# Column-wise substitution in the RWKV base blocks, and the transposes of q and k drained by ScalarE alone

## The chip, the cores and the metric

The kernel runs on one core of a Trainium2 chip. The core has five engines with instruction queues of their own: TensorE (PE; its weight loads are listed as PEld), VectorE (DVE), ScalarE (ACT), GpSimd (POOL) and SyncE (SP), which here only issues DMA transfers. The metric is the device time of one execution in microseconds; a time is the median of several executions. Beside it there is one profiled execution, whose span runs from the first to the last instruction.

## The reference

One decoder layer over 1024 prompt tokens and 8 x 8 sampled tokens: one input projection is split among an RWKV-7 group, a short convolution and stick-breaking attention, and an output projection, an MLP and a gated embedding follow. Two pieces matter here. The RWKV-7 state is a recurrence over the tokens:

```
def step(s, inp):
    r_t, w_t, k_t, v_t, a_t, b_t = inp
    sa = jnp.einsum('bhvk,bhk->bhv', s, a_t)
    s = (s * w_t[:, :, None, :] + sa[..., None] * b_t[:, :, None, :]
         + v_t[..., None] * k_t[:, :, None, :])
    y = jnp.einsum('bhvk,bhk->bhv', s, r_t)
```

And the queries and keys of the attention (8 heads of 64) are normalised and get a gain for each position in the head:

```
q = rmsnorm(q, lw['q_gain'])
k = rmsnorm(k, lw['k_gain'])
...
z = jnp.einsum('bqhd,bkhd->bhqk', q_blk.astype(jnp.float32), kf) * scale + bias_f
```

Everything is float32. TensorE's products of large matrices are made of two parts for each operand, a rounded high part and the remainder (names with h and l).

## The kernel before, in words

**The recurrence in chunks.** The 1024 tokens are 16 chunks of 64. Inside a chunk the recurrence is a unit triangular system, and the kernel inverts its matrix for each chunk and head. For a half j of the heads (two heads, j = 0 and 1), `wkv_products` makes the matrices on TensorE (L260) in three groups of 8, 8 and 1 chunks (the last is the sampled tokens), multiplies them by a triangular mask into the tile LT (VectorE, L262; two buffers), and stores them to `l_s` in memory. After j = 1, `wkv_base` loads the diagonal blocks of 32 x 32 of all 16 chunks, 4 heads and 2 blocks: 128 blocks, one on each partition, the tile base_Z (L276). The substitution that inverts them runs in VectorE: for row i a product of i x i elements (L281) into base_Q and a sum over its last axis (L283) into row i of base_X, for i from 1 to 31. One operand of the product is base_X read transposed. Then L284 writes the transposed inverse, and L285 stores both to `t_s`. The sampled tokens go through the same function later with blocks of 16.

**Around it.** For each j, the lines L425 to L443 make the remaining streams: aa and kx (L425, L426), pinv (L427, stored), r times the decay (rx, stored), rx times the bonus weights and kx (L436), and the bonus itself (L442 on TensorE, L443 on VectorE). The tiles of this phase share buffers, among them one group of 12, so a later tile waits for the last reader of an earlier one.

**The attention's projection.** `project` makes q, k and v for two halves of the heads (hf), in groups of 256 tokens (i0): 48 matmuls a group (L791 to L793) into a PSUM bank (two banks, in turn), a copy into the tile nat (ScalarE, L798; five buffers), the square (ScalarE, L801), its sum (VectorE, L803), a root and a reciprocal (L804, L805) and the product (VectorE, L806). `keep` writes k and v out (GpSimd multiplies k by its gain, L816). `stack` transposes q and k of a group on TensorE (L840, four transposes) into one PSUM bank, of which there is one; ScalarE writes the rounded high part times the gain to sth (L842), VectorE the remainder to stl (L843), and four DMA issues, two on ScalarE's queue and two on SyncE's, store them (L846). sth, stl and the tile spl of v share four buffers. There are 16 stacks, and a stack is put behind the last matmul of a later group.

**The local step of the chunks.** `wkv_local` takes the chunks in pairs: SyncE loads ar, bk (L483, L486) and TT, the blocks of `t_s` (L491). TensorE multiplies (L508) and transposes, VectorE masks (L511), L539 and L544 put the off-diagonal part together, L552 adds it into TT, and L560 and L562 apply TT. `wkv_chain` then steps over the chunks one after another (L621 to L638), and the attention follows.

**What sets the order.** The program is written as one sequence; a scheduler that simulates the times orders the instructions on each engine, and each engine then runs its own list strictly in order. A wait of one instruction holds all that stand behind it on its engine. `tc.issue_after(x)` makes the scheduler put what is inside behind the instruction x. Since TensorE can do the projection matmuls at almost any time, the scheduler puts them between the small products of the chunks.

Of the kernel before, what the change touches and what calls it, by code (L numbers as in the profile page):

```python
# [21 lines left out]
F32 = mybir.dt.float32  # L22
F32R = mybir.dt.float32r
I32 = mybir.dt.int32
AF = mybir.ActivationFunctionType
ALU = mybir.AluOpType
AX = mybir.AxisListType
# [21 lines left out]
def hybrid_step(ctx: ExitStack, tc: tile.TileContext, I, O):  # L49
    nc = tc.nc  # L50
    V, S, G, PE, SP = nc.vector, nc.scalar, nc.gpsimd, nc.tensor, nc.sync
# [4 lines left out]
    def f(t):  # L56
        return t.bitcast(F32)
# [79 lines left out]
    def P1(name, i=0):  # L137
        return par[:, col[name] + i:col[name] + i + 1]
# [42 lines left out]
    for i in range(9):  # L181
# [4 lines left out]
        xt, r = xts[i]  # L186
# [7 lines left out]
        for g in range(2):  # L194
            pt = tr().rearrange("p (k t) -> p k t", k=4)
            for k in range(4):
                c = (4 * g + k) * 128
# [19 lines left out]
    pt = tr()  # L217
# [8 lines left out]
    mfull = km.tile([128, 2, 2, 64], F32, name="mfull")  # L226
    G.memset(mfull, 1.0)
    for s in range(2):
        hs = slice(64 * s, 64 * s + 64)
        for q in range(2):  # L230
            for kind in range(2):
                m = mfull[hs, q, kind, :]
# [18 lines left out]
    def wkv_products(j, am, bm):  # L251

        for c0 in (0, 8, 16):
            n = min(8, 17 - c0)
            p3 = tr()[:, :n * 64].rearrange("p (c t) -> p c t", c=n)
            for c in range(n):
                for s in range(2):
                    hs = slice(64 * s, 64 * s + 64)
                    q = slice((c0 + c) * 64, (c0 + c) * 64 + 64)
                    PE.matmul(p3[hs, c, :], bm[hs, q], am[hs, q], start=True, stop=True)  # L260
            LT = bp.tile([128, 8, 64], F32, name="LT", bufs=2)
            V.tensor_mul(LT[:, :n], p3, mfull[:, c0 // 16, 1, None, :].to_broadcast([128, n, 64]))  # L262
            c = c0 % 16
            for s in range(2):
                SP.dma_start(l_s[c0 // 16][c:c + n, 2 * j + s].rearrange("c i t -> i c t"), LT[64 * s:64 * s + 64, :n])

    def wkv_base(pool, nc_, BS, l_s, t_s, tags=("Z", "X", "Q"), bufs=(1, 1, 1)):
        na = 64 // BS
        np_ = nc_ * 4
        P_ = slice(0, na * np_)  # L270
        Z = pool.tile([128, BS, BS], F32, name="base_Z", tag=tags[0], bufs=bufs[0])
        X = pool.tile([128, 2, BS, BS], F32, name="base_X", tag=tags[1], bufs=bufs[1])
        Q = pool.tile([128, BS * BS], F32, name="base_Q", tag=tags[2], bufs=bufs[2])
        blocks = l_s.rearrange("c h (a r) (b t) -> a b (c h) r t", a=na, b=na)
        for a in range(na):
            SP.dma_start(Z[a * np_:(a + 1) * np_], blocks[a, a])  # L276
        G.memset(X[P_, 1], 0.0)
        G.memset(X[P_, 1].rearrange("p r t -> p (r t)")[:, 0:BS * BS:BS + 1], 1.0)
        for i in range(1, BS):
            q = Q[P_, 0:i * i].rearrange("p (c j) -> p c j", c=i)  # L280
            V.tensor_mul(q, Z[P_, 0:i, i][:, None, :].to_broadcast([na * np_, i, i]),  # L281
                         X[P_, 1, 0:i, 0:i].rearrange("p j c -> p c j"))
            V.reduce_sum(X[P_, 1, i, 0:i], q, axis=AX.X)  # L283
        V.tensor_copy(X[P_, 0], X[P_, 1].rearrange("p r t -> p t r"))  # L284
        SP.dma_start(t_s.rearrange("a c h k r t -> (a c h) k r t"), X[P_])  # L285


# [2 lines left out]
    def pe_tile(name, dtype=F32):  # L290
        return rp.tile([128, LW], dtype, name=name, tag="pe", bufs=12)
# [14 lines left out]
    pt = tr()  # L306
# [7 lines left out]
    last = rp.tile([9, 1024], F32, name="last")  # L314

    def rw_tile(w, m, ct):

        raw = pe_tile("raw")
        xs = pe_tile("xs")
        G.memset(raw[:, 0:1], 0.0)  # L320
        rs3 = raw[:, E1:E1 + NB * 9].rearrange("p (b j) -> p b j", j=9)
        G.tensor_copy(rs3[:, :, 0], shT[:, ct, :])
        for t0, n in CH:
            ps = acc()
            gemm_t(ps, w, m, hT, t0, n)
            np_ = min(n, NP - t0)
            S.copy(raw[:, 1 + t0:1 + t0 + np_], ps[:, :np_])
            if np_ < n:
                S.copy(rs3[:, :, 1:9], ps[:, np_:n].rearrange("p (b j) -> p b j", j=NJ))
            S.activation(xs[:, t0:t0 + n], ps[:, :n], AF.Copy, scale=om[:, ct:ct + 1])  # L330
            V.scalar_tensor_tensor(xs[:, t0:t0 + np_], raw[:, t0:t0 + np_], P1("mu_shift", ct),
                                   xs[:, t0:t0 + np_], op0=ALU.mult, op1=ALU.add)
            if np_ < n:
                x3 = xs[:, NP:T].rearrange("p (b j) -> p b j", j=NJ)
                V.scalar_tensor_tensor(x3, rs3[:, :, 0:8], P1("mu_shift", ct), x3, op0=ALU.mult, op1=ALU.add)
        pt = tr()
        PE.transpose(pt[:9, :128], raw[:, NP:NP + 81:9], ident)
        V.tensor_copy(last[:, ct * 128:ct * 128 + 128], pt[:9, :128])
        return xs
# [24 lines left out]
    sg, aa = [], []  # L364
# [9 lines left out]
    for j in range(2):  # L374
        t_ = slice(0, T)

        kx = rw_tile(W.load(w_in[:, 256 + 128 * j:384 + 128 * j], ncol=128), 0, 2 + j)
        kn = pe_tile("kn")
        S.activation(kn[:, t_], kx[:, t_], AF.Square, scale=P1("k_k", j))

        pt = tr()
# [18 lines left out]
        for t0, n in CH:  # L400
            ps = tr()
            for t in range(t0, t0 + n, 128):
                r = min(128, T - t)
                for a in range(2):
# [3 lines left out]
                                   op1=ALU.mult)  # L408
        cum = pe_tile("cum")
        V.tensor_tensor_scan(cum[:, t_], reset, sg[j][:, t_], 0.0, op0=ALU.mult, op1=ALU.add)  # L410
        pm = sg[j]
# [7 lines left out]
        V.tensor_mul(kn[:, t_], kn[:, t_], aa[j][:, t_])  # L419
        V.tensor_mul(kn[:, t_], kn[:, t_], pinv[:, t_])  # L420
        SP.dma_start(bk_s[0, j], kn[:, t_])
        wkv_products(j, pm, kn)
        if j:
            wkv_base(bp, 16, 32, l_s[0], t_s[0])
        V.tensor_scalar(aa[j][:, t_], aa[j][:, t_], P1("k_a", j), om[:, 8 + j:9 + j], op0=ALU.mult, op1=ALU.add)  # L425
        V.tensor_mul(kx[:, t_], kx[:, t_], aa[j][:, t_])  # L426
        V.tensor_mul(pinv[:, t_], kx[:, t_], pinv[:, t_])  # L427
        SP.dma_start(bk_s[1, j], pinv[:, t_])
        S.activation(cum[:, t_], cum[:, t_], AF.Exp, scale=-C0)
# [340 lines left out]
    gainT = sbp.tile([128, 2], F32, name="gainT")  # L770
# [63 lines left out]
    def stack(hf, n, i0, nat):  # L834

        pt = tr_sb()
        p4 = pt.rearrange("p (r i t) -> p r i t", r=2, i=2)
        for r in range(2):
            for i in range(2):
                PE.transpose(p4[:, r, i, :], nat[:, i, r * 128:r * 128 + 128], ident)  # L840
        hl = [sbp.tile([128, 512], F32R, name=f"st{e}", tag="st", bufs=4) for e in "hl"]
        S.activation(hl[0], pt, AF.Copy, scale=gainT[:, n:n + 1])  # L842
        V.scalar_tensor_tensor(hl[1], pt, gainT[:, n:n + 1], f(hl[0]), op0=ALU.mult, op1=ALU.subtract)  # L843
        for e in range(2):
            for s in range(2):
                (S, SP)[e].dma_start(stk_s[n, 4 * hf + s:4 * hf + 4:2, e, :, i0 * 128:i0 * 128 + 256]  # L846
                                     .rearrange("r d t -> d r t"),
                                     f(hl[e])[64 * s:64 * s + 64].rearrange("p (r t) -> p r t", r=2))
# [3 lines left out]
    for hf in range(2):  # L852
        for n in range(3):
            w = W.load(w_in[:, SB0 + 512 * n + 256 * hf:SB0 + 512 * n + 256 * hf + 256])
            for i0 in range(0, 9, 2):
                nat, last = project(hf, n, w, i0)
# [747 lines left out]
```

## Time and profile before

| | us |
|---|---|
| three runs | 1729.45, 1730.25, 1733.58 |
| median | 1730.25 |
| profiled execution, whole | 1737.61 |
| its span | 1735.9 |
| mean granted TensorE clock in it | 0.98 |
| VectorE busy, over the span | 1116.0 |
| ScalarE busy, over the span | 774.3 |

In a row of a timeline stand the start, the duration, the engine, the line, the operation, out<-in by the program's names, the shape, the count and, in brackets, the idle time of the engine just before it with what ended it. A group has its shape and count, then the busy time of all and the mean ns of one, then the idle time before them. "PE b L840 <- DVE stl L843" means that the matmul of L840 waited for the VectorE instruction of L843. The buffers of PSUM are all called b. A profile shows a run of equal instructions at one place as one row with x2 or more.

### The profile page before, as it was taken

To read this page: it belongs to the slowest core of one execution; us is meant where nothing else is said; L and a number is where in the kernel's file an instruction comes from. 1 tells how busy PE (TensorE), PEld (TensorE's weight loads), DVE (VectorE), ACT (ScalarE), POOL (GpSimd) and SP (SyncE) were. 2 spreads that over 40 slices of the span, in tenths; PEclk is the share of its full clock that TensorE was granted. 3 is DMA by queue.
4 is the path that set the end of the run, shared out by engine and by line. 5 is a ranking of instruction groups with operands and counts; after the bars stand their busy time and mean duration, and the time that the engine had idled before them with its cause. 6 is when DMAs were issued, how large, how long until landed. Compare 5 with 4: busy or idle time off the path is not lost.

```text
span 1735.9 us, 30705 instructions
## 1 busy us (share of the span) xinstructions
PE 1660.3 (96%) x11901; PEld 1494.8 (86%) x11901; DVE 1116.0 (64%) x1840; ACT 774.3 (45%) x1537; POOL 699.0 (40%) x746
## 2 busy tenths in 40 slices
PE   6999889999999889999999999999899999999998
PEld 5898889888998667888886778988899999998898
DVE  6266863555476759888854345367877787867432
ACT  6633323323353647656543444354443434435421
POOL 4123131212341655443434653466755555635210
PEclk9999989999999899999999999999999999999999
DMA  5134456434623754334245656321332322322211
GB/s 186 48 118 128 110 153 168 120 76 128 165 87 77 252 144 133 117 111 126 76 120 158 187 170 203 93 73 49 110 95 77 98 86 88 96 86 73 64 51 40
DMA packets 207060, 197.03 MB, mean 114 GB/s; under 512 B 58113, under 2 KB 172449, under 8 KB 206786
## 3 DMA queue, kind: packets, MB, share of 16 engines
q1 hardware_dynamic: 197186, 174.08, 33.9%
q0 software_dynamic: 5120, 16.78, 3.3%
q10 hardware_dynamic: 4608, 4.20, 1.0%
q8 instruction: 94, 1.54, 0.4%
q14 instruction: 52, 0.43, 0.1%
HBM read 158.03 MB, written 36.98 MB: 112 GB/s over the span
## 4 chain that ended last, share of the span: by engine, by line
PE 74%; DVE 11%; DMA 5%; issue 3%; SPq 2%; ACT 2%; POOL 1%; ACTq 0%; DVEq 0%; POOLq 0%
PE b L1087 13%; PE b L1089 13%; PE b L1088 13%; PE b L1430 3%; PE b L1429 3%; PE b L1428 3%; PE b L169 2%; PE b L170 2%; PE b L171 2%; PE b L791 2%; PE b L792 2%; PE b L936 2%; PE b L793 2%; DVE base_Q L281 1%; DMA wr<-in_w_up 1%
## 5 line engine op out<-in xcount | busy, mean ns | idle before, releaser
L1068 POOL TENSOR_TENSOR wl<-wr,wh 128x512 fp32r<-128x512 f32 x172 | 245.1, 1432 | 289.5 <-ACT wh L1067 239.8
L1067 ACT CAST wh<-wr 128x512 fp32r<-128x512 f32 x292 | 179.6, 622 | 309.0 <-PE b L1088 205.9
L1087 PE MATMUL b<-ah,wh 128*128 128x288 f32 (+1 forms) x768 | 256.4, 334 | 11.5 <-DVE x L1466 8.8
L1466 DVE TENSOR_TENSOR x<-b,x 128x288 f32<-128x288 f32 (+1 forms) x384 | 198.7, 528 | 105.9 <-PE b L1089 103.1
L1089 PE MATMUL b<-ah,wl 128*128 128x288 f32 (+1 forms) x768 | 252.9, 329 | 0.0
L1088 PE MATMUL b<-al,wh 128*128 128x288 f32 (+1 forms) x768 | 252.5, 329 | 0.0
L1087 PEld LDWEIGHTS b<-ah,wh 128*128 128x128 f32 x768 | 145.2, 189 | 25.7 <-DVE x L1466 13.4
L1087 PE MATMUL b<-nh,wh 128*128 128x512 f32 (+1 forms) x448 | 164.9, 370 | 2.5 <-DVE x L1466 1.6
L1088 PE MATMUL b<-nl,wh 128*128 128x512 f32 (+1 forms) x448 | 165.3, 369 | 1.2 <-DVE nl L1311 1.2
L1089 PE MATMUL b<-nh,wl 128*128 128x512 f32 (+1 forms) x448 | 163.6, 365 | 0.0
L1089 PEld LDWEIGHTS b<-ah,wl 128*128 128x128 f32 x768 | 145.3, 189 | 10.5
L1088 PEld LDWEIGHTS b<-al,wh 128*128 128x128 f32 x768 | 145.3, 189 | 8.9
L791 PE MATMUL b<-wh,h_hi 128*128 128x256 f32 x432 | 130.6, 302 | 0.0
L159 POOL TENSOR_TENSOR wl<-wr,wh 128x1024 fp32r<-128x1024 f32 x26 | 69.2, 2673 | 150.3 <-ACT wh L158 150.2
L792 PE MATMUL b<-wl,h_hi 128*128 128x256 f32 x432 | 127.7, 296 | 0.0
L793 PE MATMUL b<-wh,h_lo 128*128 128x256 f32 x432 | 126.7, 293 | 0.0
L169 PE MATMUL b<-h_hi,wh 128*128 128x384 f32 (+1 forms) x336 | 115.2, 343 | 1.9 <-ACT xs L330 1.2
L170 PE MATMUL b<-h_lo,wh 128*128 128x384 f32 (+1 forms) x336 | 112.9, 336 | 0.3 <-DVE h_lo L201 0.3
L171 PE MATMUL b<-h_hi,wl 128*128 128x384 f32 (+1 forms) x336 | 111.8, 333 | 0.0
L916 DVE TENSOR_TENSOR_SCAN keep<-keep,onesq 128x128 f32<-128x128 f32 (+3 forms) x64 | 94.7, 1480 | 25.4 <-POOL keep L914 25.1
L1068 DVE TENSOR_TENSOR wl<-wr,wh 128x512 fp32r<-128x512 f32 x120 | 103.0, 861 | 9.8 <-ACT wh L1067 5.9
L1068 POOL TENSOR_TENSOR wsl<-s,wsh 128x512 fp32r<-128x512 f32 x64 | 88.6, 1407 | 29.6 <-ACT wsh L1067 29.5
(421 smaller groups left out, 4332.6 us busy)
## 6 DMA issues: line engine op xcount, KB each, us to landing
wr<-in_w_up SPq DMA_DIRECT2D x64, 512.0 KB
wr<-in_w_down SPq DMA_DIRECT2D x64, 512.0 KB
wr<-in_w_in SPq DMA_DIRECT2D x26, 512.0 KB
wr<-in_w_out SPq DMA_DIRECT2D x16, 512.0 KB
xt<-in_x_prompt SPq DMA_DIRECT2D x8, 512.0 KB
stk_s<-sth ACTq DMA_DIRECT2D x32, 128.0 KB
stk_s<-stl SPq DMA_DIRECT2D x32, 128.0 KB
v_s<-spl SPq DMA_DIRECT2D x16, 256.0 KB
```

Of the source, the lines that this page charges most:

```text
L169: PE.matmul(ps[:, :n], wh[:, k, c], a, start=(k == 0), stop=False)
L170: PE.matmul(ps[:, :n], wh[:, k, c], b, start=False, stop=False)
L171: PE.matmul(ps[:, :n], wl[:, k, c], a, start=False, stop=(k == nk - 1))
L791: PE.matmul(o, a, w[0][:, k, :], start=(k == 0), stop=False)
L792: PE.matmul(o, a, w[1][:, k, :], start=False, stop=False)
L793: last = PE.matmul(o, b, w[0][:, k, :], start=False, stop=(k == 7))
L1067: S.copy(h3, src)
L1068: (sub or G).tensor_sub(l3, src, f(h3))
L1087: PE.matmul(ps[:, :n], w(0, k, m), a, start=(k == 0), stop=False)
L1088: PE.matmul(ps[:, :n], w(0, k, m), b, start=False, stop=False)
L1089: PE.matmul(ps[:, :n], w(1, k, m), a, start=False, stop=(k == nk - 1))
L1466: V.tensor_add(p.x[:, m, t0:t0 + n], ps[:, :n], p.x[:, m, t0:t0 + n])
```

## The change

It has three parts. The arithmetic of the results is the same up to the order of additions and roundings.

1. `wkv_base` updates by columns. When row j of the inverse is final, its product with the elements of Z below it, (31 - j) rows of (j + 1) elements, goes to base_Q (the new L284) and is added in place to the rows j + 1 to 31 of base_X (the new L286). The steps run over j from 0 to 30. base_Q has a quarter of its size, since (31 - j)(j + 1) is at most 256. The transposed copy goes from VectorE to ScalarE (the new L287).
2. `wkv_products` gives back the last LT product, and the product of kx and aa (L426 before, L430 now) is put behind it; L427 and L436, which read kx, come later with it.
3. `stack` lets ScalarE write the transposes times the gain from PSUM into nat, the tile that they were made from (the new L846); ScalarE rounds that to sth (L848), and VectorE subtracts the two, both in SBUF (L849).

```diff
-            V.tensor_mul(LT[:, :n], p3, mfull[:, c0 // 16, 1, None, :].to_broadcast([128, n, 64]))
+            last = V.tensor_mul(LT[:, :n], p3, mfull[:, c0 // 16, 1, None, :].to_broadcast([128, n, 64]))
...
+        return last
...
-        Q = pool.tile([128, BS * BS], F32, name="base_Q", tag=tags[2], bufs=bufs[2])
+        Q = pool.tile([128, BS * BS // 4], F32, name="base_Q", tag=tags[2], bufs=bufs[2])
...
-        for i in range(1, BS):
-            q = Q[P_, 0:i * i].rearrange("p (c j) -> p c j", c=i)
-            V.tensor_mul(q, Z[P_, 0:i, i][:, None, :].to_broadcast([na * np_, i, i]),
-                         X[P_, 1, 0:i, 0:i].rearrange("p j c -> p c j"))
-            V.reduce_sum(X[P_, 1, i, 0:i], q, axis=AX.X)
-        V.tensor_copy(X[P_, 0], X[P_, 1].rearrange("p r t -> p t r"))
+        for j in range(BS - 1):
+            n, m = BS - 1 - j, j + 1
+            q = Q[P_, 0:n * m].rearrange("p (r c) -> p r c", r=n)
+            V.tensor_mul(q, Z[P_, j, m:BS, None].to_broadcast([na * np_, n, m]),
+                         X[P_, 1, None, j, 0:m].to_broadcast([na * np_, n, m]))
+            V.tensor_add(X[P_, 1, m:BS, 0:m], X[P_, 1, m:BS, 0:m], q)
+        S.copy(X[P_, 0], X[P_, 1].rearrange("p r t -> p t r"))
...
-        wkv_products(j, pm, kn)
+        last_l = wkv_products(j, pm, kn)
...
-        V.tensor_mul(kx[:, t_], kx[:, t_], aa[j][:, t_])
+        with tc.issue_after(last_l.ins):
+            V.tensor_mul(kx[:, t_], kx[:, t_], aa[j][:, t_])
...
+        raw = nat.rearrange("p i c -> p (i c)")
+        S.activation(raw, pt, AF.Copy, scale=gainT[:, n:n + 1])
         hl = [sbp.tile([128, 512], F32R, name=f"st{e}", tag="st", bufs=4) for e in "hl"]
-        S.activation(hl[0], pt, AF.Copy, scale=gainT[:, n:n + 1])
-        V.scalar_tensor_tensor(hl[1], pt, gainT[:, n:n + 1], f(hl[0]), op0=ALU.mult, op1=ALU.subtract)
+        S.copy(hl[0], raw)
+        V.tensor_sub(hl[1], raw, f(hl[0]))
```

Lines behind `wkv_base` move by three, behind the change of kx by four, and behind `stack` by six: L443 becomes L447, L552 becomes L556, L560 becomes L564. Since the scheduler orders by its own times, the lists of the engines change as far as the middle of the program, well beyond these lines. Three places follow.

VectorE at the end of the second half (j = 1), before; xs is the shared buffer of kx, rx and the others:

```order
L425 TENSOR_SCALAR aa<-aa,par,om 128x1088
L331 SCALAR_TENSOR_TENSOR xs<-raw,par,xs 128x384
L426 TENSOR_TENSOR xs<-xs,aa 128x1088
L427 TENSOR_TENSOR pinv<-xs,pinv 128x1088
L436 SCALAR_TENSOR_TENSOR xs<-xs,par 128x1088
L262 TENSOR_TENSOR LT<-b_1278,mfull 128x512
L331 SCALAR_TENSOR_TENSOR xs<-raw,par,xs 128x256
L335 SCALAR_TENSOR_TENSOR xs<-raw,par,xs 128x64
L262 TENSOR_TENSOR LT<-b_1299,mfull 128x512
L338 COPY last<-b_1603 9x128
L443 TENSOR_TENSOR xs<-b_1607,xs 128x384
L262 TENSOR_TENSOR LT<-b_1320,mfull 128x64
```

and there now:

```order
L428 TENSOR_SCALAR aa<-aa,par,om 128x1088
L334 SCALAR_TENSOR_TENSOR xs<-raw,par,xs 128x384
L262 TENSOR_TENSOR LT<-b_1278,mfull 128x512
L334 SCALAR_TENSOR_TENSOR xs<-raw,par,xs 128x256
L338 SCALAR_TENSOR_TENSOR xs<-raw,par,xs 128x64
L262 TENSOR_TENSOR LT<-b_1299,mfull 128x512
L341 COPY last<-b_1603 9x128
L262 TENSOR_TENSOR LT<-b_1320,mfull 128x64
L430 TENSOR_TENSOR xs<-xs,aa 128x1088
L431 TENSOR_TENSOR pinv<-xs,pinv 128x1088
L440 SCALAR_TENSOR_TENSOR xs<-xs,par 128x1088
L284 TENSOR_TENSOR base_Q<-base_Z,base_X 128x31
```

The three LT products moved ahead of the three long products, and the first base step stands behind these; the L443 (now L447) stand among the base steps. On TensorE the same move puts 76 projection matmuls between the products of `wkv_products` and L442 (L446 now), where 25 stood.

SyncE around the store of the base blocks, before:

```order
L285 DMA t_s<-base_X 128x2048
L846 DMA stk_s<-stl 64x2x256 x2
L824 DMA out<-nat 128x2x256
L824 DMA out<-kg 128x2x256
L820 DMA new_70<-kg 64x256
L822 DMA out<-kg 64x256
L832 DMA v_s<-spl 128x4x128
L483 DMA ar<-ar_s 128x3x64 x2
L486 DMA ar<-ar_s 128x2x64 x3
```

and there now, with the rows behind the loads:

```order
L288 DMA t_s<-base_X 128x2048
L852 DMA stk_s<-stl 64x2x256 x2
L487 DMA ar<-ar_s 128x3x64 x2
L490 DMA ar<-ar_s 128x2x64 x3
...
L495 DMA TT<-t_s 32x8x32 x4
L591 DMA gt<-g_s 128x2x128
L593 DMA bt<-bon_s 128x2x128
L487 DMA bk<-bk_s 128x2x64 x2
L490 DMA bk<-bk_s 128x2x64 x2
L828 DMA out<-kg 128x2x256 x2
L852 DMA stk_s<-stl 64x2x256 x3
```

Of the first eight stacks, the stores of seven stood ahead of the loads of the chunk pairs; now those of four stand behind the loads of the first three pairs. VectorE's rows at the first pairs are now these:

```order
L515 TENSOR_TENSOR AB<-b_1646,mfull 128x4x128
L809 RECIPROCAL ss<-ss 128x8
L543 TENSOR_TENSOR LM<-AB,lvl 64x256 x2
L810 TENSOR_TENSOR nat<-nat,ss 128x512
L807 TENSOR_REDUCE ss<-sq 128x4
L849 TENSOR_TENSOR stl<-nat,sth 128x512
L809 RECIPROCAL ss<-ss 128x4
L810 TENSOR_TENSOR nat<-nat,ss 128x256
L835 TENSOR_TENSOR spl<-nat,spl 128x4x64
L556 TENSOR_TENSOR TT<-b_1695,TT 128x4x64
```

A subtraction of `stack` (L849) stands there between L543 and L556, whose forerunners L539 and L552 stood next to each other. On TensorE 530 projection matmuls stand ahead of the first L564, where 699 stood ahead of L560.

ScalarE at the end of the base, now:

```order
L802 COPY nat<-b_3422 128x512
L805 ACTIVATE sq<-b_3422 128x512
L808 ACTIVATE ss<-ss,eps_rms 128x8
L287 COPY base_X<-base_X 128x1024
L802 COPY nat<-b_3483 128x512
L805 ACTIVATE sq<-b_3483 128x512
L846 ACTIVATE nat<-b_3544,gainT 128x512
L848 CAST sth<-nat 128x512
```

The copy L287, which stood in VectorE's list as L284, stands ahead of the seventh group's copy and square and of the fourth stack's drain.

## The prediction

> **What bounds the kernel now.** I read the page first: busy times, then the chain that ended last.
>
> ```profile
> span 1735.9 us, 30705 instructions
> PE 1660.3 (96%) x11901; PEld 1494.8 (86%) x11901; DVE 1116.0 (64%) x1840; ACT 774.3 (45%) x1537; POOL 699.0 (40%) x746
> PE 74%; DVE 11%; DMA 5%; issue 3%; SPq 2%; ACT 2%; POOL 1%; ACTq 0%; DVEq 0%; POOLq 0%
> ```
>
> TensorE is busy for 1660.3 of 1735.9 us. None of its matmuls is removed, so the change can gain only what TensorE loses by waiting, or by the lower clock that follows a wait. The base blocks, the masks of LT and most stacks run between 160 and 300 us; the two largest waits of TensorE there are these (released line, releaser, total us, times, longest us), and behind them the stretches (PE, PEld, DVE, ACT, POOL busy, granted clock, DMA share, GB/s).
>
> ```profile
> PE b L840 <- DVE stl L843: 10.0, 3, 5.0
> PE b L442 <- DVE LT L262: 3.5, 1, 3.5
> ```
>
> ```profile
> 180.00:200.00 20.00, 18.88 (x155) 18.28 (x154) 19.41 (x46) 7.45 (x15) 1.81 (x1) 1.00 0.26 63
> 200.00:220.00 20.00, 14.94 (x117) 14.53 (x116) 19.83 (x25) 5.81 (x12) 6.31 (x4) 0.90 0.41 114
> 220.00:240.00 20.00, 18.63 (x145) 18.38 (x144) 19.93 (x21) 7.07 (x15) 8.88 (x5) 0.93 0.45 116
> 260.00:300.00 40.00, 39.29 (x398) 36.26 (x398) 12.93 (x31) 13.16 (x28) 5.32 (x3) 0.96 0.72 183
> ```
>
> VectorE is full from 180 to 240 us (19.41, 19.83, 19.93 of 20). There it sets the pace: the transposes of a stack (L840) wait for the bank that L843 of the stack before has still to read, and L843 stands in VectorE's queue between base steps. From 260 us TensorE is the bound again.
>
> **What can be had.** The timeline of TensorE shows two of the waits and what follows the first.
>
> ```profile
> 218.24 1.11 PE L840 MATMUL b<-ident,nat 128*128 128x128 f32 x4 [5.02 <-DVE stl L843]
> ...
> 219.57 0.41 PE L791 MATMUL b<-wh,h_hi 128*128 128x256 f32 x1
> 219.79 0.41 PE L792 MATMUL b<-wl,h_hi 128*128 128x256 f32 x1
> ...
> 222.92 0.28 PE L792 MATMUL b<-wl,h_hi 128*128 128x256 f32 x1
> 223.03 0.28 PE L793 MATMUL b<-wh,h_lo 128*128 128x256 f32 x1
> ...
> 243.06 0.94 PE L840 MATMUL b<-ident,nat 128*128 128x128 f32 x4 [4.43 <-DVE stl L843]
> ```
>
> The two groups above sum to 13.5 us, and the long ones are three: 5.02 and 4.43 here, and 3.5 ahead of L442. After such a wait projection matmuls start 0.22 us apart (219.57, 219.79), from 4.5 us on 0.11 to 0.12 apart (222.92, 223.03). So some 16 to 20 matmuls lose 0.1 us each, 1.6 to 2.0 us a wait, about 6 for three. **About 20 us** (13.5 and 6) is the ceiling.
>
> **Part 1, the turned substitution.** What goes is one row of each group (the last is a single copy):
>
> ```profile
> L281 DVE TENSOR_TENSOR base_Q<-base_Z,base_X 128x1 f32<-128x1 f32 (+30 forms) x31 | 26.9, 868 | 4.2 <-DMA base_Z<-l_s 3.6
> L283 DVE TENSOR_REDUCE base_X<-base_Q 128x1 f32<-128x1 f32 (+30 forms) x31 | 15.5, 501 | 0.6
> L284 DVE COPY base_X<-base_X 128x1024 f32<-128x1024 f32 x1 | 2.0, 2020 | 0.0
> ```
>
> 26.9 + 15.5 + 2.0 = 44.4 us of VectorE. In their place come 31 multiplies and 31 additions of (31-j)(j+1) elements, 5456 each, 10912 together. Their price is the timeline's, for products of two SBUF operands:
>
> ```profile
> 177.81 0.16 DVE L281 TENSOR_TENSOR base_Q<-base_Z,base_X 128x1 f32<-128x1 f32 x1 [3.56 <-DMA base_Z<-l_s]
> 178.01 0.15 DVE L283 TENSOR_REDUCE base_X<-base_Q 128x1 f32<-128x1 f32 x1
> ...
> 183.20 0.69 DVE L806 TENSOR_TENSOR nat<-nat,ss 128x512 f32<-128x512 f32 x1
> ...
> 206.55 0.42 DVE L806 TENSOR_TENSOR nat<-nat,ss 128x256 f32<-128x256 f32 x1
> ...
> 233.04 1.96 DVE L281 TENSOR_TENSOR base_Q<-base_Z,base_X 128x961 f32<-128x961 f32 x1
> ```
>
> 256 more elements cost 0.27 us, 1.05 ns an element above 0.155; dependent steps start 0.04 later than the one before ends (177.97 to 178.01). That is 62 x 0.19 + 10912 x 0.00104 = **23.1 us**, 21 less. The old multiply paid (1.96 - 0.16) / 961 = 1.9 ns an element for its transposed operand; a walk down a column of Z might keep that in the new multiply, and the sum would then be 23.1 + 5456 x 0.0009 = 28; both kinds at 2.04 (1.96 over 961, nothing off) give 34. I take 23.1, since L806 has a broadcast operand as the new steps have; 34 stays the dear end. The copy goes to ScalarE, which passes 1024 elements of a weight in 1.05 us:
>
> ```profile
> 157.22 1.05 ACT L158 CAST wh<-wr 128x1024 fp32r<-128x1024 f32 x1 [0.76 <-DMA wr<-in_w_in]
> ```
>
> Its read is transposed, so it lies between that and L284's 2.02; I take 1.5.
>
> **Part 2, kx behind the last LT.** L262 stood behind 8 us of VectorE:
>
> ```profile
> 158.29 3.36 DVE L427 TENSOR_TENSOR pinv<-xs,pinv 128x1088 f32<-128x1088 f32 x1
> 161.57 3.43 DVE L436 SCALAR_TENSOR_TENSOR xs<-xs,par 128x1088 f32<-128x1088 f32 x1
> 164.93 0.68 DVE L262 TENSOR_TENSOR LT<-b,mfull 128x512 f32<-128x512 f32 x1
> ...
> 169.37 0.23 DVE L262 TENSOR_TENSOR LT<-b,mfull 128x64 f32<-128x64 f32 x1 [1.46 <-DMA l_s<-LT]
> ```
>
> The third LT ends 3.99 us after the first one's end (165.61 to 169.60), held by the first one's transfer; the base starts 8.2 us after the third (177.81). With the first LT at about 157.6, where L426 stood, its end is 158.3, the third's 162.3 and the base starts near 170.5. Meanwhile the three deferred operations (1.27 + 3.36 + 3.43) fill 162.3 to 170.4, so they cost the base nothing. TensorE's wait of 3.5 goes, but L442 needs L436's output and now comes some 5 us later: the order puts 76 projection matmuls ahead of it instead of 25, 51 x 0.12 = 6 us, enough. The square of the second projection group (its buffer is that of the last L443) then waits behind L443, which stands among base steps: I estimate 2.3 us of TensorE, from 0 to 2.6 (what ScalarE waited there before).
>
> **Part 3, ScalarE empties the transposes.** Sixteen L842 and L843 go:
>
> ```profile
> L842 ACT ACTIVATE sth<-b,gainT 128x512 fp32r<-128x512 f32 x8 | 5.5, 686 | 6.0 <-PE b L840 6.0
> L843 DVE SCALAR_TENSOR_TENSOR stl<-b,gainT,sth 128x512 fp32r<-128x512 f32 x8 | 5.9, 743 | 2.4 <-DMA stk_s<-stl 2.4
> ```
>
> A bank is free after one ScalarE pass of 0.69 us and not after L843. VectorE pays 0.69 (L806's row) for 0.743, no gain. ScalarE gets a second pass, 0.6 to 0.7 each, 16 in all: it is busy 45% and not on the path here.
>
> **When the base ends.** The order puts these among the base steps: 14 operations of 512 elements (L803, L806 and the new L849) that give way to the next after some 0.6 us each, a half one (0.3), three L443 (0.56) and six L805 (0.15), 11.3 us. These rows price a clash with GpSimd:
>
> ```profile
> 198.19 5.22 POOL L159 TENSOR_TENSOR wl<-wr,wh 128x1024 fp32r<-128x1024 f32 x2 [34.33 <-ACT wh L158]
> 198.26 2.88 DVE L806 TENSOR_TENSOR nat<-nat,ss 128x512 f32<-128x512 f32 x1
> ...
> 201.40 2.84 DVE L281 TENSOR_TENSOR base_Q<-base_Z,base_X 128x441 f32<-128x441 f32 x1
> 204.27 0.61 DVE L283 TENSOR_REDUCE base_X<-base_Q 128x21 f32<-128x441 f32 x1
> ```
>
> While L159 ran, L806 took 2.88 for 0.69 and L281 2.84 for about 1.0 (441 elements at 1.9 ns, and 0.16): 4.0 us for this pair. 170.5 + 23.1 + 11.3 + 4.0 = **208.9**, against 240.9 before (L284's row ended at 240.94).
>
> The Trainium skill, "SBUF — State Buffer", section "Who interferes with whom", says that a VectorE instruction with two SBUF inputs contends with a GpSimd instruction that reads SBUF, and one with at most one SBUF input does not. Both rows above agree, and L843, with one input in PSUM, never took over 0.753 us. By that rule the change exposes more: L283, with one input, becomes an addition with two, and L843 a subtraction with two. By the rule each meeting costs about 2 us.
>
> **What is late next.** The copy L287 stands in ScalarE's queue ahead of the seventh group's copies and the fourth stack's drain, so a bank that TensorE wants at about 208.6 (161.9, 324 projection matmuls at 0.12, 4 for L442 and the transposes, 4 for the wait in part 2 with its slow clock) is free only after the copy, the group's two passes and the drain (208.9 + 1.5 + 0.6 + 0.6 + 0.5): about 212.1, so 3.5 us, and 1.7 of slow clock. Then SyncE:
>
> ```profile
> 240.96 0.34 SPq L285 DMA_DIRECT2D t_s<-base_X  x1
> 243.03 1.25 SPq L846 DMA_DIRECT2D stk_s<-stl  x2
> ...
> 248.55 1.04 SPq L483 DMA_DIRECT2D ar<-ar_s  x2
> ...
> 273.65 1.83 SPq L846 DMA_DIRECT2D stk_s<-stl  x2
> ```
>
> The loads of three chunk pairs and their neighbours took from 248.55 to 273.65, 25.1 us. In the new order they follow t_s and two stores of the fourth stack at once, so they start near 215 and end near 240. Behind them wait the stores of stack 5. Its tiles are two of four, so L849 of stack 7 waits for them, and VectorE's next local step (L556, once L552) stands a few rows behind that L849. A store lands about 2 us after its issue (243.03 + 1.25 to 246.23, when the L843 that waited for one began), so: 240.4 + 1.3 + 2.0 = 243.7, then 0.7 and 0.43, and TensorE's L560 at about **246**, 37 us behind the base's end. Here TensorE runs out of projection matmuls: in its order only 530 of them stand ahead of L560, 699 before.
>
> ```profile
> 273.37 0.33 PE L560 MATMUL b<-X,TT 64*64 64x64 f32 x4
> ```
>
> Before, L560 was reached at 273.37 with 169 more projections done, worth 169 x 0.12 = 20.2 us. 246.1 + 20.2 = 266.3: a gain of 7.1 us; the slow clock after this new wait takes 1.5 of it. So of the ceiling of 20, about 14 goes into new waits (2.3 + 5.2 + some 5 + 1.5) and **5.6** stays. Later TensorE has fillers enough in both orders, and what follows moves with it. The profiled execution took 1737.6 (span 1735.9 and 1.7 around it); 1737.6 - 5.6 = 1732.0. It lies 7.4 above the median of the runs, 1730.25, and I take the same off there: 1730.25 - 5.6 = **1724.7**.
>
> **The rivals.**
>
> - A, full recovery: the stores of stack 5 slip between the loads or TensorE's fillers cover the wait, and only the 20 us counts: 1710. For it: SP's two engine waits before were short, and the base ends 32 us earlier. Against: the printed order.
> - C, the port takes it: two more meetings with L159 or L816 (1.9 to 2.2 each, POOL is busy 8.1 us between 180 and 220) push the base's end 4 us later, one to one: 1728.7. The rule named above is for it.
> - D, slower: VectorE isn't relieved. If column steps cost 2.04 ns (34 us, +10.9) and the longer stay meets GpSimd twice more (+4), the base ends at 224, L560 comes at 261, and 5.6 - 14.9 = -9.3: 1739.5. It turns slower from a base end at 214.5 on, and measurably at 220. For it: L281's 1.96 at 961 elements. Against: 1.04 ns for L806.
>
> **How the numbers follow.** A 0.26, forecast 0.40, C 0.20, D 0.14. A run of this kernel can tell 0.3% (5.2 us) from nothing, so faster is below 1725.1: A, somewhat over half of the forecast (it lies at the edge) and a little of C, 0.52; slower is most of D and its nearest neighbours, 0.13; the same is 0.35. The range takes in A with 2 us beyond it and C, and reaches into D: 1708 to 1735.
>
> **What would show it.** Right: the base from 170 to about 209 with steps up to 256 elements at 0.42; no wait of L844 for VectorE's stl; instead one near 209 for ScalarE, and idle before L564 (now L560's line) near 240 with L849 waiting for stk_s. Wrong: base steps over 0.5 us for 256 elements, L849 at 2 us in many places, or no idle before L564.

## The result, and the profile after

| | before | after | ratio (95% interval) |
|---|---|---|---|
| median of five runs | 1730.25 us | 1720.23 us | 0.9925 (0.9898 to 0.9952) |
| the same once more, later | 1737.39 us | 1725.32 us | 0.9928 (0.9906 to 0.9949) |

The ratio with its interval is the recorded one and not the quotient of the two medians, which differ by 10.0 and 12.1 us. The change gains 0.7%, some 10 to 13 us. The profiled execution of after took 1714.58 us, the fastest of its five, and that of before (1737.61) was slower than all five of before; so the two pages differ by 23 us of span, which is more than the medians do, and it isn't known where in before's profile its extra time lies. The profile of the repeat (span 1724.9) is used as a check.

The page of after, the lines that answer to those of before:

```profile
span 1712.8 us, 30734 instructions
PE 1644.8 (96%) x11901; PEld 1484.3 (87%) x11901; DVE 1089.7 (64%) x1838; ACT 787.9 (46%) x1555; POOL 695.2 (41%) x746
PE 77%; DVE 9%; DMA 6%; ACT 3%; issue 3%; SPq 2%; POOL 1%; ACTq 0%; POOLq 0%; DVEq 0%
```

Again the same 11901 matmuls, and TensorE is busy 96% of the span. VectorE lost 26 us and ScalarE gained 14. The waits of TensorE from 160 to 300 us, after (released line, releaser, us, times, longest):

```profile
PE b L795 <- ACT sq L805: 5.0, 1, 5.0
PE b L512 <- DMA bk<-bk_s: 2.2, 1, 2.2
PE b L844 <- ACT nat L846: 0.9, 1, 0.9
```

In the repeat:

```profile
PE b L795 <- ACT sq L805: 5.3, 1, 5.3
PE b L512 <- DMA bk<-bk_s: 2.1, 1, 2.1
PE b L844 <- ACT nat L846: 0.7, 1, 0.7
```

The waits for stl (10.0 us) and for LT (3.5 us) are gone. In their place stand the three rows above, 8.1 us together. The timeline of VectorE, after, shows the base:

```profile
168.46 0.19 DVE L284 TENSOR_TENSOR base_Q<-base_Z,base_X 128x31 f32<-128x31 f32 x1 [6.27 <-DMA base_Z<-l_s]
...
182.77 0.42 DVE L284 TENSOR_TENSOR base_Q<-base_Z,base_X 128x256 f32<-128x256 f32 x1
183.23 0.42 DVE L286 TENSOR_TENSOR base_X<-base_X,base_Q 128x256 f32<-128x256 f32 x1
...
192.54 2.48 DVE L286 TENSOR_TENSOR base_X<-base_X,base_Q 128x207 f32<-128x207 f32 x1
195.06 2.44 DVE L284 TENSOR_TENSOR base_Q<-base_Z,base_X 128x192 f32<-128x192 f32 x1
...
204.38 0.19 DVE L286 TENSOR_TENSOR base_X<-base_X,base_Q 128x31 f32<-128x31 f32 x1
```

It runs from 168.46 to 204.57 us, where before it took from 177.81 to 240.94. A step of 256 elements takes 0.42 us. Two steps met GpSimd (L159, from 192.29 on) and took 2.48 and 2.44 us.

From here on three stretches are compared, cut at marks in TensorE's own work, with nearly the same number of recorded matmuls between them (the second number in brackets) before and after: the first product of `wkv_products` (L260), the last L717 of the sampled tokens (L721 after), and the first L1193 (L1199 after). A row has the stretch, its length, busy us of PE, PEld, DVE, ACT and POOL with the instructions, the granted clock, the DMA share and GB/s. Before:

```profile
110.50:502.40 391.90, 375.45 (x3682) 346.24 (x3681) 231.91 (x439) 132.48 (x275) 102.60 (x106) 0.97 0.48 129
502.40:914.10 411.70, 395.56 (x2204) 332.29 (x2206) 320.26 (x469) 238.74 (x483) 174.63 (x256) 0.98 0.43 128
914.10:1735.90 821.80, 794.97 (x5501) 730.37 (x5500) 507.77 (x855) 338.07 (x663) 388.58 (x322) 0.99 0.33 99
```

After:

```profile
106.40:487.40 381.00, 366.05 (x3666) 339.43 (x3667) 208.43 (x432) 142.05 (x285) 96.78 (x103) 0.98 0.48 131
487.40:895.20 407.80, 392.99 (x2212) 332.36 (x2216) 314.37 (x471) 243.04 (x490) 176.79 (x260) 0.98 0.44 131
895.20:1712.80 817.60, 794.02 (x5507) 729.14 (x5506) 511.27 (x857) 337.93 (x663) 388.09 (x322) 0.99 0.33 100
```

And the first stretch of the repeat:

```profile
109.40:490.90 381.50, 366.42 (x3667) 339.64 (x3667) 209.03 (x432) 142.06 (x285) 97.01 (x103) 0.98 0.48 131
```

The first stretch is 10.9 us shorter (10.4 in the repeat). Only 1.5 us of that is idle time of TensorE (391.90 - 375.45 = 16.45; 381.00 - 366.05 = 14.95); 9.4 us is busy time of nearly the same work. With the granted clock taken in steps of 5 us, the lower clock cost 13.7 us in this stretch before and 8.5 after, so 5.2 of the 9.4 are clock. A single profile says little about the clock: over the whole kernel and all executions of the repeat it cost 27.9 us on average (each time multiplied by what its granted clock lacks to 1), in before's beside them 31.0, so some 3 us of the gain. Another 2.3 us are no gain: 14 matmuls of the attention and the convolution, which before has at the end of this stretch (from 493.0 to 500.8 us), come behind its mark after. Nor did the projection matmuls become quicker: from one to the next 0.132 us pass on average in both. What the rest of the busy time is, some 2 us, the runs don't settle.

### The profile page after: what moved, and what is told of

It is laid out like the page before. It is cut to its first block, busy times and chain, and to the rows that moved or that the text cites. A ratio compares the mean times of both kernels' runs of the same rounds, so it can differ in the third digit from the quotient of the medians.

```text
span 1712.8 us, 30734 instructions
## 1 busy us (share of the span) xinstructions
PE 1644.8 (96%) x11901; PEld 1484.3 (87%) x11901; DVE 1089.7 (64%) x1838; ACT 787.9 (46%) x1555; POOL 695.2 (41%) x746
## 4 chain that ended last, share of the span: by engine, by line
PE 77%; DVE 9%; DMA 6%; ACT 3%; issue 3%; SPq 2%; POOL 1%; ACTq 0%; POOLq 0%; DVEq 0%
PE b L1093 13%; PE b L1094 13%; PE b L1095 13%; PE b L1436 3%; PE b L1435 3%; PE b L1434 3%; PE b L169 3%; PE b L170 3%; PE b L171 3%; PE b L797 2%; PE b L795 2%; PE b L796 2%; PE b L942 1%; DVE keep L922 1%; PE b L512 1%
## 5 line engine op out<-in xcount | busy, mean ns | idle before, releaser
L1074 POOL TENSOR_TENSOR wl<-wr,wh 128x512 fp32r<-128x512 f32 x172 | 240.0, 1404 | 268.3 <-ACT wh L1073 248.4
L1095 PEld LDWEIGHTS b<-ah,wl 128*128 128x128 f32 x768 | 144.9, 189 | 10.2
L795 PE MATMUL b<-wh,h_hi 128*128 128x256 f32 x432 | 127.0, 294 | 5.0 <-ACT sq L805 5.0
L159 POOL TENSOR_TENSOR wl<-wr,wh 128x1024 fp32r<-128x1024 f32 x26 | 64.7, 2503 | 120.5 <-ACT wh L158 120.5
```

The lines of the kernel that those rows point to most:

```text
L795: PE.matmul(o, a, w[0][:, k, :], start=(k == 0), stop=False)
L1074: (sub or G).tensor_sub(l3, src, f(h3))
L1095: PE.matmul(ps[:, :n], w(1, k, m), a, start=False, stop=(k == nk - 1))
```

## The experiments

Each was timed beside the kernel before, on the same chip. The edit is against the changed kernel unless it says otherwise.

**The changed kernel again.** No edit.

> The changed kernel once more, beside the others on the same chip, since taking out any one of its parts cost the whole gain. If the gain is real it stays 8 to 14 us below before; if the five runs so far were a lucky draw it comes out within 5 us. In the profile the new waits are at the places of the first one: some 5 us of a projection matmul for the square, 1 to 3 us at the first local products, none of a transpose for stl.

Ratio 0.9928 (0.9906 to 0.9949). The gain stands, and the waits are in their places.

**Without the turned substitution.**

```diff
-        for j in range(BS - 1):
...
-        S.copy(X[P_, 0], X[P_, 1].rearrange("p r t -> p t r"))
+        for i in range(1, BS):
...
+        V.tensor_copy(X[P_, 0], X[P_, 1].rearrange("p r t -> p t r"))
```

> The change without its first part: rows, sums and VectorE's transposed copy as before, with kx behind the last LT and with ScalarE emptying the transposes. Theory V (VectorE's relief by the turned substitution makes the gain): the base ends near 235 us again, TensorE waits some 8 us or more for VectorE (for nat instead of stl) between 180 and 245, and the time is within 3 us of before. Rival D (the gain comes from the bank, which no longer waits for a VectorE instruction): TensorE waits for VectorE less than 3 us there although the base is as long as before, and the time is 7 to 13 us below before, as with the whole change.

Ratio 1.0002 (0.9982 to 1.0021): nothing of the gain is left. The waits of TensorE, 150 to 300 us:

```profile
PE b L793 <- ACT sq L803: 6.3, 2, 4.7
PE b L842 <- DVE nat L808: 3.6, 2, 2.4
PE b L575 <- DVE AB L513: 1.5, 1, 1.5
PE b L553 <- ACT Y L548: 1.3, 1, 1.3
```

The base ends at 229.1. TensorE waits 5.1 us for VectorE itself (nat, AB), less than theory V said and more than D said, and the long wait for the square stays. The time is the one that V said: the drain and the earlier LT gain nothing without the turned substitution.

**Without kx behind the last LT.**

```diff
-        with tc.issue_after(last_l.ins):
-            V.tensor_mul(kx[:, t_], kx[:, t_], aa[j][:, t_])
+        V.tensor_mul(kx[:, t_], kx[:, t_], aa[j][:, t_])
```

> The change without its second part: kx is not put behind the last LT. Theory V and rival D alike: the wait of TensorE's bonus product for LT returns (3.5 us and 2 of slow clock), but the bonus products then stand ahead of the base steps, so the 5.0 us wait of a projection matmul for the square goes with its 2 us of slow clock: about the time of the whole change, 8 to 14 us below before. If the second part were worth more than that exchange, it would be 5 us or less below before.

Ratio 1.0022 (1.0001 to 1.0043). The expected exchange of waits came, and yet the gain went; both theories missed; what came is the third case of the expectation, 5 us or less below before. In its trace:

```profile
PE b L444 <- DVE LT L262: 3.4, 1, 3.4
PE b L510 <- DMA bk<-bk_s: 2.1, 1, 2.1
PE b L842 <- DVE nat L808: 1.8, 1, 1.8
```

The base starts at 178.25 instead of 168 to 172 and ends at 217.8. The wait for the square is gone, but this order of the engines is no better than before's: the first stretch takes 392.2 us.

**Without ScalarE's drain.**

```diff
-        raw = nat.rearrange("p i c -> p (i c)")
-        S.activation(raw, pt, AF.Copy, scale=gainT[:, n:n + 1])
...
-        S.copy(hl[0], raw)
-        V.tensor_sub(hl[1], raw, f(hl[0]))
+        S.activation(hl[0], pt, AF.Copy, scale=gainT[:, n:n + 1])
+        V.scalar_tensor_tensor(hl[1], pt, gainT[:, n:n + 1], f(hl[0]), op0=ALU.mult, op1=ALU.subtract)
```

> The change without its third part: sth by ScalarE and stl by VectorE, both out of the bank, as before. Theory V: VectorE is no longer full while the stacks run, so the waits of the transposes for stl shrink from 10.0 us to 2 or less, and the time is 8 to 13 us below before. Rival D: the transposes wait 6 us or more for stl among the base steps, and the time is at most 5 us below before.

Ratio 1.0006 (0.9986 to 1.0026). The waits of TensorE, 150 to 300 us:

```profile
PE b L795 <- ACT sq L805: 5.2, 1, 5.2
PE b L844 <- DVE stl L847: 2.2, 1, 2.2
```

The transposes wait for stl once, 2.2 us, about as V said; but the time is before's, which V had not. The first stretch does take only 385.3 us, 6.6 less than before, and the second gives 4.1 back (411.7 before):

```profile
493.70:909.50 415.80, 396.99 (x2208) 332.79 (x2208) 318.14 (x471) 244.11 (x491) 171.41 (x260) 0.98 0.43 128
```

There TensorE idles 18.8 us (415.80 - 396.99), before 16.1, in many waits of at most 3 us. The orders of the engines differ there too, and why this one is worse stays open.

**The base behind the bonus.** The base steps are put behind the last L447, so that the bonus products don't wait among them.

```diff
-        if j:
-            wkv_base(bp, 16, 32, l_s[0], t_s[0])
...
-            V.tensor_mul(rx[:, t0:t0 + n], ps[:, :n], vx[:, t0:t0 + n])
+            bon = V.tensor_mul(rx[:, t0:t0 + n], ps[:, :n], vx[:, t0:t0 + n])
+        if j:
+            with tc.issue_after(bon.ins):
+                wkv_base(bp, 16, 32, l_s[0], t_s[0])
```

> The whole change, with the base steps put behind the last bonus product of VectorE (its own order only). Both theories: the projection matmul that waited 5.0 us for the square, and that for the last bonus product among the base steps, waits less than 1 us, and the 2 us of slow clock behind it go: some 6 us below the whole change, 15 to 19 us below before. If the wait was only the first of two for the same thing (the load of the base blocks), another takes its place and the time is that of the whole change.

Ratio 0.9946 (0.9927 to 0.9964), near the changed kernel's; the intervals overlap. The timeline of TensorE shows the two places:

```profile
170.60 0.39 PE L796 MATMUL b<-wh,h_hi 128*128 128x256 f32 x1 [0.19 <-ACT sq L806]
181.73 1.11 PE L845 MATMUL b<-ident,nat 128*128 128x128 f32 x4 [5.12 <-DVE nat L811]
```

The wait for the square fell from 5.0 to 0.19, and the first transposes wait 5.12 for nat: it was the first of two.

**The squares in memory of their own.**

```diff
+    sqp = tc.alloc_tile_pool(name="sqp", bufs=1, side="right", reuse_waits="tile")
...
-            sq = sbp.tile([128, 512], F32, name="sq", bufs=1)
+            sq = sqp.tile([128, 512], F32, name="sq", bufs=1)
```

> The changed kernel with the tile of the squares in memory of its own, where it takes no bonus tile's place. TensorE's order is that of the changed kernel word for word. Theory M (the square waits only for that memory): the wait of 5.0 us goes. Then two cases. M1: nothing else was late, TensorE gains 5 us and 2 of slow clock, 6 to 8 us below the changed kernel. M2: the normalised nat of the first stack stands behind some twelve base steps on VectorE, as the run with the base behind the bonus showed (5.1 us there); the wait moves to the first transposes, 3 to 5 us, and the time is within 3 us of the changed kernel.

Ratio 0.993 (0.9911 to 0.995), the changed kernel's: the second case, M2. The timeline of TensorE:

```profile
182.33 1.11 PE L845 MATMUL b<-ident,nat 128*128 128x128 f32 x4 [5.96 <-DVE nat L811]
```

So the square waited only for the memory of a bonus tile, and without that wait nat is late by about as much.

**The copy back on VectorE.**

```diff
-        S.copy(X[P_, 0], X[P_, 1].rearrange("p r t -> p t r"))
+        V.tensor_copy(X[P_, 0], X[P_, 1].rearrange("p r t -> p t r"))
```

> The changed kernel with the transposed copy of the base back on VectorE. Its own cost is the 0.9 us wait of a transpose for the drain behind that copy, and 2 us of VectorE. Theory P (the gain comes from the waits named, not from the order as such): the time is within 4 us of the changed kernel. Theory O (the order that the scheduler happens to find is worth as much as the parts): the time may fall anywhere between before and the changed kernel, with waits after 300 us that neither has.

Ratio 0.9942 (0.992 to 0.9963): within 4 us of the changed kernel, as P says, though O would allow that too. The place of the copy isn't what gains.

**The turned substitution alone**, against before: the first part of the change.

> Before with the turned substitution alone. If the parts add up, their sum being about 10 us and no part missing costing less than 9, it is within 5 us of before, since the waits for LT (3.5 us) and for stl (some 2 us or more) stay. If the turned substitution carries the gain by itself it is 8 us or more below before.

Ratio 1.0025 (1.001 to 1.004), slower by 4 us, within the 5 expected. L444 waits 3.2 us for LT, and the base starts at 178.1.

**The drain alone**, against before: the third part of the change.

> Before with the third part alone, ScalarE emptying the transposes. The 10.0 us of transposes that wait for stl go; with VectorE as full as before they wait for nat instead (3 us or more), and L442 still waits 3.5 us for LT. If waits were all that counts, 3 to 7 us below before; as the parts taken out one at a time left nothing of the gain, within 4 us of before.

Ratio 1.001 (0.9993 to 1.0028). The waits:

```profile
PE b L442 <- DVE LT L262: 3.5, 1, 3.5
PE b L791 <- ACT sq L801: 2.7, 1, 2.7
PE b L508 <- DMA bk<-bk_s: 2.6, 1, 2.6
PE b L840 <- DVE nat L806: 2.1, 3, 0.9
```

The 10.0 us for stl are gone, and others came, for the square and the loads; the base ends at 236.9.

**kx behind the last LT alone**, against before: the second part of the change.

> Before with the second part alone, kx behind the last LT. The 3.5 us wait for LT and its slow clock go, a wait of some 5 us for the square comes, and the waits for stl stay: within 4 us of before.

Ratio 0.9983 (0.9967 to 0.9998), some 3 us faster. The wait for LT is gone, 4.7 for the square and 5.8 for stl are there.

**Each multiply twice.** The second writes the same values again.

```diff
-            V.tensor_mul(q, Z[P_, j, m:BS, None].to_broadcast([na * np_, n, m]),
-                         X[P_, 1, None, j, 0:m].to_broadcast([na * np_, n, m]))
+            for _ in range(2 if BS == 32 else 1):
+                V.tensor_mul(q, Z[P_, j, m:BS, None].to_broadcast([na * np_, n, m]),
+                             X[P_, 1, None, j, 0:m].to_broadcast([na * np_, n, m]))
```

> The changed kernel with each multiply of the 32-row substitution issued twice (the second writes the same again): some 12.5 us more of VectorE in the base and nothing else. The scheduler then puts TensorE's chain products back behind as many projection matmuls as in before (699 ahead of the first L564). Theory V (the length of the base on VectorE is what counts): at least half of the gain goes, 0 to 6 us below before. Rival (the length is covered, the drain by ScalarE and the earlier LT carry the gain): still 9 us or more below before.

Ratio 1.0018 (1.0002 to 1.0034): the whole gain is gone, as theory V said and a little more. The base ends at 232.8, later than the 12.5 us of the extra multiplies would put it, since the order also changed; so this run holds length and order together. But in its profile the gain isn't lost ahead of the products that read the base. As in before, 699 projection matmuls stand ahead of the first product with TT (L560 before, L565 here), so the stretches from the first L260 to it, and from it to the last L717 (L722 here), hold the same work. Before:

```profile
110.50:273.37 162.87, 148.10 (x1207) 142.67 (x1207) 111.12 (x162) 51.54 (x95) 45.89 (x27) 0.95 0.49 131
273.37:502.40 229.03, 227.35 (x2476) 203.57 (x2475) 120.79 (x277) 80.94 (x181) 56.72 (x79) 0.98 0.48 127
```

With each multiply twice:

```profile
110.17:262.90 152.73, 143.24 (x1208) 139.32 (x1207) 102.73 (x192) 57.65 (x104) 40.69 (x27) 0.98 0.51 138
262.90:503.30 240.40, 235.01 (x2473) 209.78 (x2474) 124.73 (x276) 86.29 (x189) 59.04 (x79) 0.94 0.46 121
```

In spite of the longer steps the first product with TT comes some 10 us earlier than in before, as far ahead as in the changed kernel (the table below). Behind it 11.4 us are lost, most of them by a granted clock of 0.94, and 8.9 more in the second stretch (420.6 us). This profile was the slowest of its twelve executions (1743.36, median 1737.02), so not all of that is the kernel's. Why the clock was lower there stays open.

**Squares and gains early, and the store from ScalarE.** Over the run with the squares' own memory, the gains' loads and scalings stand at the start in the same pool:

```diff
-        SP.dma_start(t_s.rearrange("a c h k r t -> (a c h) k r t"), X[P_])
+        S.dma_start(t_s.rearrange("a c h k r t -> (a c h) k r t"), X[P_])
...
-    gains = sbp.tile([128, 2, 64], F32, name="gains")
-    gainT = sbp.tile([128, 2], F32, name="gainT")
+    gains = sqp.tile([128, 2, 64], F32, name="gains")
+    gainT = sqp.tile([128, 2], F32, name="gainT")
```

> The changed kernel with the tile of the squares in memory of its own, the two gains loaded and scaled at the start, and the store of the base blocks issued by ScalarE behind its copy. TensorE's order is that of the changed kernel word for word. With the squares alone in their own memory the wait only moved to the first transposes (6.0 us, for nat, which stood behind a scaling that waited 2.5 us for the gains' load). If that load was the last thing late, the wait there falls to 3 us or less and the time is 2 to 5 us below the changed kernel, 14 to 17 below before. If nat stands behind the base steps anyway, the wait stays 4 us or more and the time is the changed kernel's.

Ratio 0.9905 (0.9886 to 0.9924), 16 us below before, as in the first case of the expectation. It has the lowest ratio of all, but its interval overlaps the changed kernel's, so that it beats it is likely and not shown. The wait stayed as in the second case: 5.9 us for nat, whose sum of squares stood behind the first base steps:

```profile
178.41 0.68 DVE L808 TENSOR_REDUCE ss<-sq 128x8 f32<-128x512 f32 x1
179.01 0.38 DVE L295 TENSOR_TENSOR base_Q<-base_Z,base_X 128x220 f32<-128x220 f32 x1
```

The square was ready long before that (at 163.35); nine pairs of base steps (from 171.66 on) stand ahead of its sum.

**Together.** Between the first L260 and the first L564 (or its like) TensorE has the same 507 other recorded matmuls in every kernel; only the number of projection matmuls ahead of L564 differs. "Ahead at L564" is how much sooner after the first L260 it comes than in before, less 0.12 us for each projection matmul that is then still to do, an estimate with the prediction's price (with 0.132, the mean above, it is up to some 2 us less). "Behind it" is what the time from there to the third stretch adds to that or, with a minus, takes back.

| kernel | parts | base ends, us | projections ahead of L564 | ahead at L564, us | behind it, us | ratio |
|---|---|---|---|---|---|---|
| before | none | 240.9 | 699 | 0 | 0 | 1 |
| kx only | 2 | 228.5 | 642 | 6.9 | -3.3 | 0.9983 |
| drain only | 3 | 236.9 | 693 | 0.2 | -0.7 | 1.0010 |
| turned only | 1 | 218.5 | 557 | 9.1 | -11.3 | 1.0025 |
| no drain | 1, 2 | 209.4 | 522 | 10.6 | -8.1 | 1.0006 |
| no kx | 1, 3 | 217.8 | 563 | 8.9 | -13.3 | 1.0022 |
| no turn | 2, 3 | 229.1 | 638 | 7.7 | -3.1 | 1.0002 |
| after | 1, 2, 3 | 206.7 | 530 | 9.8 | 5.0 | 0.9925 |
| after, repeat | 1, 2, 3 | 209.6 | 530 | 9.9 | 3.0 | 0.9928 |
| multiplies twice | 1, 2, 3 | 232.8 | 699 | 10.2 | -20.3 | 1.0018 |

The end of the base includes its copy. The two columns before the ratio come from one profile of each kernel, and executions of one kernel spread by some 10 us.

The parts don't add up: alone they give -0.17%, +0.10% and +0.25%, together -0.75%. With all three, the base ends before 214 us in every kernel that gained; an early end alone isn't enough (no drain). Every kernel but that with the drain only is some 7 to 11 us ahead at L564, also those that gained nothing. Whether that lasts is decided behind it, well past the base: those without a gain (and kx only, with its small one) lose 3 to 20 us there, the changed kernel and its four other variants lose at most 2.6 or win up to 7.5. The groups lie close at their border, given the spread. What in the order of the engines behind L564 makes the difference, no run isolates.

## Why the prediction came out so

The forecast was 1724.7 with a range of 1708 to 1735; measured 1720.23 (0.9925). The sign and the range were right, and the gain was 10 to 13 us where 5.6 was forecast. By its own steps:

- **The price of the new steps** was right: 0.42 us for 256 elements as L806's row had said, and 12.5 + 13.2 = 25.7 us busy for 62 steps with two long meetings with GpSimd in them, some 28 with the 0.04 us between steps; 23.1 + 4.0 was forecast. The dear end (2 ns an element, rival D) isn't seen.
- **The base's end** was forecast at 208.9 and was 204.6, in the repeat 207.5; the copy took 2.1 us more, 1.5 was forecast. The start at 170.5 was 168.46 and 171.47: the third LT ended at 158.40 already, but the base came 10.1 us behind it and not 8.2. But the first L260 came 4.0 us earlier in this profile than in before's, and 1.0 in the repeat. Counted from it, the base ends after 98.1 and 98.0 us, forecast 98.4. The three deferred operations took 1.27, 1.29 and 1.35 us, not 3.4, since no L159 ran beside them any more: in before the last two had met GpSimd (156.59 to 163.85), and their rows held a price that wasn't theirs.
- **The wait for the square** was forecast at 2.3 us (from 0 to 2.6) and was 5.0 and 5.3. It was bounded by what ScalarE had waited there before (2.56). Now ScalarE stood idle for 11.3 us there until the last L447 had ended, and TensorE came to the place 5 us ahead of it:

```profile
171.14 0.60 ACT L805 ACTIVATE sq<-b 128x512 f32<-128x512 f32 x1 [11.30 <-DVE xs L447]
171.78 0.58 PE L795 MATMUL b<-wh,h_hi 128*128 128x256 f32 x1 [5.00 <-ACT sq L805]
```

The run with the squares' own memory shows that it hides a second one as long, nat behind the base steps.
- **The bank behind the copy** was forecast at 3.5 us and was 0.9 and 0.7. The wait for the loads of bk (2.2 and 2.1) wasn't in the sum.
- **The step that failed** is the last one, the wait ahead of L564: some 5 us of TensorE and 1.5 of slow clock, because L849 of stack 7 was to wait for the stores of stack 5. The timeline of VectorE, after:

```profile
227.61 1.53 DVE L849 TENSOR_TENSOR stl<-nat,sth 128x512 fp32r<-128x512 f32 x1 [1.72 <-ACT sth L848]
...
236.34 0.42 DVE L556 TENSOR_TENSOR TT<-b,TT 128x256 f32<-128x256 f32 x1 [3.87 <-DMA gt<-g_s]
```

That of SyncE, the stores of stack 5 and the first of stack 6:

```profile
238.50 1.91 SPq L852 DMA_DIRECT2D stk_s<-stl  x3
```

That of ScalarE, the high part of stack 8:

```profile
247.36 0.62 ACT L848 CAST sth<-nat 128x512 fp32r<-128x512 f32 x1 [4.42 <-DMA stk_s<-stl]
```

And that of TensorE:

```profile
239.23 0.33 PE L564 MATMUL b<-X,TT 64*64 64x64 f32 x4
```

SyncE issued the stores of stack 5 at 238.50, as late as forecast (240.4). But stack 7's L849 began at 227.61, eleven us earlier, so the tile that it writes was not one of those that wait there; I had counted the four buffers off in turn. The wait fell on stack 8 (4.42 us of ScalarE), whose L849 stands behind L556, and TensorE came to L564 at 239.23 with no idle time in front, not at 246. Without these 6.5 us the sum gives 12.1, which is near what was measured; that it is so near is partly luck, since the errors above go both ways. Counted from the first L260, L564 comes after 132.8 us in both profiles, 2.8 sooner than forecast (246.1 - 110.5 = 135.6). By the forecast's own reckoning the gain there is then 7.1 + 2.8 = 9.9 us, and nothing is taken off for a slow clock. What came on top was won behind L564, where the forecast let everything move along.

- **The premise** that only waits and the clock behind them can be gained isn't confirmed. Idle time fell by 6.5 us from 160 to 300 us (14.6 to 8.1, by the waits), but rose behind it, by this wait above all, which before doesn't have:

```profile
PE b L942 <- DVE beta L924: 3.5, 1, 3.5
```

Over the first stretch 1.5 us are left. Over the first two stretches, after is 14.9 us shorter and the repeat 12.8: 2.8 and 4.3 of it are idle time, 5.1 and 1.7 clock. Some 7 us in both are busy time that no row explains; before's profile was 7.4 us above its median, so part of them may be chance.

- **The rivals.** A (all of the 20 us) and D (slower) didn't come. C's mechanism is there, two base steps at 2.4 us, one at 0.86, and behind the base L849 at up to 2.54; in the base the meetings cost some 4.7 us, where the forecast had 4.0 and C twice that.
- **The Trainium skill's rule** ("SBUF — State Buffer", "Who interferes with whom") agrees with the trace at the places where it was weighed: the additions L286 (2.48 beside L159, 0.38 for as many elements at 174.91) and the subtractions L849 (from 0.63 to 2.54) are slowed, which the sums L283 (1.14 us for 961 elements beside L159) and the PSUM reader L843 (0.753 at most) weren't. A meeting with L159 cost 2.1 us in the base and from 0.9 to 1.9 for L849, and the gain was large enough to pay for them.

## What to carry to other kernels

Before summing up what a shorter stage brings, follow each wait that the change adds to the buffer or queue that makes it, by the tile that is written and not by a count in turn; one wrong tile took 6.5 us out of a sum that would have come to 12.1. Where a scheduler orders the engines by its own times, the worth of an edit isn't a property of the edit: three edits, each worth about nothing alone, were worth 0.7% together, so they have to be timed together and taken out one at a time. Being ahead at one place isn't a gain yet: variants that gained nothing were as far ahead at L564, and lost it in the new order behind. And a wait that goes may hide a second one of the same length, as the square hid nat: a look at what the waiting engine would need next shows it.

## What the runs showed of the hardware

The same kernel's profiled executions spread by more than half of the effect in places that the change doesn't touch: the third stretch took 817.6 us in one profile of the changed kernel and 824.7 in the other, with the same engine orders, and before's median was 1731 us on one chip, 1732 on a second and 1737 on a third. What is compared must come from the same chip, and parts of it from stretches that are cut at the same work. And a duration in a profile may be that of a meeting: L427 took 3.36 us beside GpSimd and its successor L431 1.29 us without, for the same 1088 elements.
